# Attention scores in four array quadrants, and weight casts of the opening ordered behind the cast of h

## The chip, the cores and the metric

The kernel runs as one program on one core of a Trainium2 chip. The metric is the device time of one execution in microseconds (us); lower is better. Times of several executions are given as their median.

## The reference, cut to what matters

One layer of a hybrid decoder on 512 tokens of width 2048, all in float32: a conditioning vector scales and shifts the normalized input, one wide projection feeds two branches (sliding-window attention and a gated delta rule), and the branches are merged and projected back.

```python
mod = silu(c) @ w_ada + b_ada                       # 2048 -> 3 x 2048
shift, scale, gate = split(mod, 3)
h = rms_norm(x, norm_w) * (1 + scale) + shift       # 512 x 2048
aq, ak, av, ag, d_qkv, dz, db, da, mg_a, mg_b = split(h @ w_in)

# attention: 32 query heads, 4 key/value heads, head size 64, window of 128 tokens
aq, ak = rope(rms_norm(aq)), rope(rms_norm(ak))
s = einsum(q, k_of_this_and_the_previous_block) / 8 # blocks of 128 queries, 256 keys
s = where(0 <= q_pos - k_pos < 128, s, -inf)        # 128 keys are valid for each query
p = exp(s - m); denom = sum(p) + exp(sink - m)
a_out = (p / denom) @ v * silu(ag)

# gated delta rule: beta = sigmoid(db), g from da, 64-token chunks (not touched)
y = sigmoid(mg_a) * (a_out @ w_o_swa) + sigmoid(mg_b) * (dn_out @ w_o_dn)
return x + gate * (y @ w_out)
```

## The kernel before, in words

**Products.** TensorE does every large product with `float32r` operands: each matrix is split into a high part (a cast to `float32r`) and a low part (what the cast left off), and a product is three matmuls of 128x512, high by high, high by low and low by high (`mm3`, lines 259, 260 and 261). Weights come in halves of up to 1024 columns: `split_half` casts the raw half on ScalarE (`whi`, line 61) and subtracts on VectorE (`wlo`, line 62). Three pairs of `whi` and `wlo` and two raw buffers exist. Matmuls of plain float32 operands are run by the hardware in two passes each, so the profile counts two instructions for each of them.

**The opening** (`startup`). It walks over the 16 slices `kt` of the model width, called steps here. For a step it needs `shift` and `scale` of 128 channels. Each is a sum over 2048 conditioning inputs: TensorE does one of the two in even steps (and in the last), by 16 matmuls of 32 columns (line 449) and a column sum (line 455); VectorE does the rest (`wa`, line 458), so one sum in an even step and two in an odd one. ScalarE makes from both `sh` (lines 468 and 471), from it `h` (line 475), and casts that to `hh` (line 476). VectorE subtracts to get `hl` (line 480). Then TensorE adds the step's products into seven banks: two tiles of attention values (`v`), a 64-column tile with the inputs of beta and the decay (`ba`), and four key tiles of the delta rule (`k`). So a step has 21 matmuls. Its weights are half of a `w_st` block of 1664 columns: 832 columns per step. The sums' weights, 2 MB for each step, come from HBM all along.

**What sets the order.** A scheduler of the framework puts the instructions of each engine in a fixed order when the kernel is built, and each engine works through its own list; across engines only semaphores order the work. `behind(a, b)` forces `a` to come later than `b` in that list. In the kernel before, the low parts of the weights (`wlo`) are put behind the step's last VectorE sum; the casts `whi` are free, and the scheduler puts them where a buffer is free.

**Attention** (`attention`, `group`, `attend`). Its small work is laid between the large products of the attention's own query and gate channels, so that TensorE never stops. For each of 4 key/value heads and each of 4 blocks of 128 tokens, `attend` makes the scores of 8 query heads (two pairs `pp`, in each two tiles `S`, one for each half `e` of the partitions), picks for each query its 128 valid keys out of the own and the previous block with a mask (lines 1424, 1426, 1429), and takes maximum, exponential and sum. The trick of the kernel: exactly 128 keys are valid for a query, so both blocks' scores share one 128x128 tile. It is transposed (`pP`), multiplied by two 0/1 masks `parts` into `pT` of the previous and the own block (line 1464), and multiplied by the values into `O` (line 1474). Score matmuls have 64 rows and 128 columns of stationary queries; `O` has 128 rows and 64 columns of stationary values for each head.

## Time and profile before

| | before |
|---|---|
| times of three executions | 2849.0 (median), 2845.32, 2851.39 us |
| the profiled execution | 2842.31 us, span of its profile 2840.5 us |
| TensorE (PE) busy | 2812.2 us, 99% of the span |
| VectorE (DVE) busy | 1940.2 us, 68% |
| ScalarE (ACT) busy | 1195.2 us, 42% |
| GpSimd (POOL) busy | 146.9 us, 5% |
| DMA | 603.30 MB, mean 212 GB/s |
| stretch of the opening's products | about 31 to 125 us |
| stretch of the attention's small work | about 572 to 1021 us |

Busy times are sums over instructions of an engine; a PE that is busy may still work at less than its peak, because an instruction's record runs from its start to its modelled end and matmuls overlap. So the distance from one start to the next tells what a matmul costs. PEld is the loading of stationary operands, which overlaps PE.

### The profile page before, as it was taken

The numbers are of one execution on the slowest core, as the hardware profiler recorded it, in microseconds if no ns is written. First come the engines' busy times: TensorE is split into PE (matmuls) and PEld (weight loads), VectorE is DVE, ScalarE is ACT, GpSimd is POOL, SyncE is SP. The second block draws the span as 40 slices with busy tenths as digits, with TensorE's granted clock in tenths as the row PEclk, the third lists the DMA queues.
The fourth block names the chain that finished last, engine by engine and source line by source line (L and its number), as shares of the span: only waits on it lengthen the run. The fifth ranks groups of instructions, "written<-read, shape, count | busy, mean of one in ns | idle before, by whom it ended". The sixth has DMA issues, their size and how long they took to land.

```text
span 2840.5 us, 38583 instructions
## 1 busy us (share of the span) xinstructions
PE 2812.2 (99%) x14312; PEld 2305.0 (81%) x14312; DVE 1940.2 (68%) x3142; ACT 1195.2 (42%) x2452; POOL 146.9 (5%) x124
## 2 busy tenths in 40 slices
PE   8999999999999999999999999999999999999999
PEld 5788888887787888888888888888888888888887
DVE  7866776867757666778766666666656766664676
ACT  5555443244454343433434333333334554432443
POOL 0010100100000010000001000000000000000000
PEclk9999999999999999999999999999999999999999
DMA  9878764322244253366777666666646887885684
GB/s 404 333 230 238 255 223 143 110 91 92 80 118 137 87 167 105 116 209 218 243 259 262 231 223 241 230 231 235 242 167 233 300 311 246 303 276 179 245 312 172
DMA packets 228368, 603.30 MB, mean 212 GB/s; under 512 B 76210, under 2 KB 102450, under 8 KB 187858
## 3 DMA queue, kind: packets, MB, share of 16 engines
q1 hardware_dynamic: 228180, 600.83, 62.2%
q8 instruction: 113, 1.85, 0.3%
q14 instruction: 75, 0.61, 0.1%
HBM read 480.35 MB, written 118.17 MB: 211 GB/s over the span
## 4 chain that ended last, share of the span: by engine, by line
PE 94%; DVE 2%; DMA 2%; ACT 1%; issue 1%; SPq 0%; POOL 0%; DVEq 0%; ACTq 0%; POOLq 0%
PE mm L259 22%; PE mm L261 21%; PE mm L260 21%; PE m L260 5%; PE m L259 5%; PE m L261 5%; PE S L1416 1%; PE pv L960 1%; PE O L1474 1%; PE pod L979 1%; PE pod L978 1%; PE pod L975 1%; PE pp L950 1%; DMA E<-g_rows 1%; PE k L259 1%; PE k L260 1%
## 5 line engine op out<-in xcount | busy, mean ns | idle before, releaser
L259 PE MATMUL mm<-hh,whi 128*128 128x512 f32 x2784 | 1129.1, 406 | 0.0
L261 PE MATMUL mm<-hh,wlo 128*128 128x512 f32 x2784 | 1089.2, 391 | 0.0
L260 PE MATMUL mm<-hl,whi 128*128 128x512 f32 x2784 | 1086.4, 390 | 0.0
L62 DVE TENSOR_TENSOR wlo<-raw,whi 128x1024 fp32r<-128x1024 f32 (+1 forms) x532 | 653.2, 1228 | 438.1 <-ACT whi L61 432.4
L61 ACT CAST whi<-raw 128x1024 fp32r<-128x1024 f32 (+1 forms) x532 | 555.9, 1045 | 838.3 <-PE mm L260 595.5
L261 PEld LDWEIGHTS mm<-hh,wlo 128*128 128x128 f32 x2784 | 522.5, 188 | 113.8 <-issue 0.4
L259 PEld LDWEIGHTS mm<-hh,whi 128*128 128x128 f32 x2784 | 523.4, 188 | 111.7 <-issue 10.6
L260 PEld LDWEIGHTS mm<-hl,whi 128*128 128x128 f32 x2784 | 524.0, 188 | 100.8 <-issue 1.6
L1225 DVE TENSOR_TENSOR q<-q,q 128x1024 f32<-128x1024 f32 x96 | 124.8, 1300 | 0.7 <-issue 0.6
L773 ACT ACTIVATE E<-E,neg_g 128x128 f32<-128x128 f32 x256 | 80.9, 394 | 90.5 <-POOL E L767 78.9
L810 DVE TENSOR_TENSOR A<-A,atmp 128x62 f32<-128x62 f32 (+30 forms) x124 | 109.2, 881 | 0.4
L802 DVE TENSOR_TENSOR atmp<-A 128x62 f32<-128x62 f32 (+30 forms) x124 | 107.4, 866 | 0.3
L907 POOL TENSOR_TENSOR qe<-qe,yq 128x512 f32<-128x512 f32 x32 | 55.6, 1755 | 920.1 <-DMA qe<-eg_rows 532.2
L980 ACT COPY osb<-pod 128x256 f32<-128x256 f32 x64 | 23.8, 372 | 152.6 <-PE pod L979 152.6
L767 POOL TENSOR_SCALAR_AFFINE_SELECT E<-E 128x512 f32<-128x512 f32 x64 | 59.3, 941 | 433.2 <-DMA E<-g_rows 241.5
L962 ACT COPY vn<-pv 128x256 f32<-128x256 f32 x64 | 23.8, 372 | 124.4 <-PE pv L960 124.4
L631 DVE SCALAR_TENSOR_TENSOR yv<-mm,convh,yv 128x511 f32<-128x511 f32 (+2 forms) x96 | 71.2, 742 | 1.1
L967 DVE TENSOR_SCALAR vs<-vn,kd 128x128 f32<-128x128 f32 x96 | 23.1, 283 | 58.3 <-ACT vn L962 58.3
L1444 ACT ACTIVATE sm<-sm,mx,rs 128x128 f32<-128x128 f32 x128 | 61.5, 482 | 3.0 <-DVE mx L1439 3.0
L990 DVE SCALAR_TENSOR_TENSOR S<-S,egl,pod 128x128 f32<-128x128 f32 x64 | 19.2, 342 | 51.0 <-ACT junk L983 51.0
L636 ACT ACTIVATE th<-yv 128x512 f32<-128x512 f32 x32 | 20.2, 631 | 76.3 <-DVE yv L631 73.7
L458 DVE SCALAR_TENSOR_TENSOR wa<-wa,silu_cb 128x2048 f32<-128x2048 f32 x22 | 50.1, 2283 | 0.0
(438 smaller groups left out, 3661.4 us busy)
## 6 DMA issues: line engine op xcount, KB each, us to landing
raw<-in_w_ch SPq DMA_DIRECT2D x158, 1024.0 KB
wa<-in_w_ada_ss SPq DMA_DIRECT2D x32, 1024.0 KB
q<-in_w_od SPq DMA_DIRECT2D x64, 512.0 KB
g_d<-q SPq DMA_DIRECT2D x64, 512.0 KB
raw<-g_d SPq DMA_DIRECT2D x32, 1024.0 KB
raw<-in_w_od SPq DMA_DIRECT2D x24, 1024.0 KB
gw<-in_w_ada_gate SPq DMA_DIRECT2D x16, 1024.0 KB
E<-g_rows SPq DMA_DIRECT2D x64, 256.0 KB
```

The lines of the kernel that those rows point to most:

```text
L61: h = self.nc.scalar.copy(out=hi, in_=src)
L62: l = self.nc.vector.tensor_tensor(out=lo, in0=src, in1=hi.bitcast(F32), op=ALU.subtract)
L259: nc.tensor.matmul(ps, lhsT=wh, rhs=xh, start=first, stop=False)
L260: nc.tensor.matmul(ps, lhsT=wh, rhs=xl, start=False, stop=False)
L261: self.last_mm = nc.tensor.matmul(ps, lhsT=wl, rhs=xh, start=False, stop=last)
L631: nc.vector.scalar_tensor_tensor(out=y[:, s:], in0=ps[:, : T - s], scalar=w[:, j : j + 1], in1=y[:, s:], op0=ALU.mult, op1=ALU.add)
L767: self.last_mask = self.nc.gpsimd.affine_select(out=E, in_=E, pattern=[[0, NTB], [1, P]], compare_op=ALU.is_ge, fill=NEG, base=0, channel_ ...
L773: self.nc.scalar.activation(E[:, c, :], E[:, c, :], AF.Exp, bias=self.neg_g[:, c, h : h + 1])
L802: eng.tensor_tensor(out=t, in0=A[:, m : m + 1, m + 1 :].to_broadcast([P, m, n]), in1=A[:, :m, m : m + 1].to_broadcast([P, m, n]), op=ALU.mult,
L810: self.behind(eng.tensor_tensor(out=A[:, :m, m + 1 :], in0=A[:, :m, m + 1 :], in1=t, op=ALU.add))
L1225: self.behind(nc.vector.tensor_tensor(out=q[f], in0=q[x], in1=q[y], op=ALU.add))
L1444: nc.scalar.activation(t, t, AF.Exp, scale=r[:, h : h + 1], bias=mx[:, h : h + 1], accum_out=den[:, h : h + 1])
```

## The change

Five edits, made together:

1. **`ba` in two matmuls.** The columns of `w_st` are put in another order, so that `ba` is last. For the 832-column halves the low part of the 64 `ba` columns is written behind the high part into the same tile `whi` (columns 832 to 895). One matmul of 128 columns then makes high by high in partitions 0 to 63 and low by high in 64 to 127; a second one of 64 columns adds high by low. The two halves are added later in `gates`, by one more VectorE instruction. A step has 20 matmuls instead of 21.
2. **The split of those halves.** Instead of one subtraction of 832 columns, VectorE does one of 768 and one of 64.
3. **The order of the split.** After the first step, the cast `whi` of a step's weights is put behind the cast `hh` of the same step on ScalarE, and both subtractions behind the step's last VectorE sum.
4. **Scores in quadrants.** For the three later blocks of tokens, each score matmul (64 rows, 128 columns, 256 keys) becomes two with 64 rows, 64 columns and 192 keys, one for each half `u` of the queries, which write partitions 0 to 63 and 64 to 127. The scores that both halves have in the same columns are copied at once; two predicated copies of 64 partitions follow instead of one of 128.
5. **Values for four heads.** `O` is made with 512 columns at a time, one matmul for each half `e` and each block of keys (4 in a later block of tokens instead of 16), with the same stationary values. `pT` of the own block is now the transposed tile less `pT` of the previous block, so one mask is left.

```diff
@@ split_half
+            src = raw[:, (n % 2) * w : (n % 2 + 1) * w]
+            if w < 1024:
+                h = self.nc.scalar.copy(out=hi[:, :w], in_=src)
+                sub = lambda out, s: self.nc.vector.tensor_tensor(
+                    out=out, in0=src[:, s], in1=hi[:, s].bitcast(F32), op=ALU.subtract
+                )
+                wide, ba = slice(0, 6 * P), slice(6 * P, w)
+                l = sub(lo[:, wide], wide)
+                low = (l, sub(hi[:, w : w + 2 * VH], ba))
...
             if self.split_behind:
-                self.behind(l, self.split_behind)
+                self.behind(h, self.split_behind[0])
+                for i in low if self.split_behind[1] else ():
+                    self.behind(i, self.split_behind[1])
@@ startup, products
-            for ps, o, n in outs:
+            for i, (ps, o, n) in enumerate(outs):
+                if i == 2:
+                    pair = [(P, x[0]), (2 * VH, x[1])]
+                    for m, xm in pair[::-1] if l else pair:
+                        nc.tensor.matmul(
+                            acc_ba[:m], lhsT=wh[:, 6 * P : 6 * P + m], rhs=xm, start=f and m == P, stop=l and m == P
+                        )
@@ startup, the loop over kt
-            self.split_behind = last_sum.get(kt + 1)
+            self.split_behind = (made["h"], last_sum.get(kt + 1))
@@ gates
-        nc.vector.tensor_copy(out=bd, in_=pb)
+        nc.vector.tensor_copy(out=bd, in_=pb[:, :, 0 : 2 * VH])
+        nc.vector.tensor_tensor(out=bd, in0=pb[:, :, 2 * VH :], in1=bd, op=ALU.add)
@@ attend, scores
-                        nc.tensor.matmul(
-                            ps[:, j, k0:], lhsT=qs[2 * pp + j][b, isl], rhs=kd[b, (i - 1) * P + k0 : (i + 1) * P],
-                            start=True, stop=True,
-                        )
+                        for u in range(2):
+                            rr = slice(u * HD, (u + 1) * HD)
+                            o = u * HD
+                            nc.tensor.matmul(
+                                ps[rr, j, HD - o : 256 - o], lhsT=q[b, i * P + o : i * P + o + HD],
+                                rhs=kd[b, (i - 1) * P + o : (i - 1) * P + o + 192], start=True, stop=True,
+                            )
...
-                        nc.vector.copy_predicated(out=t, mask=mask.bitcast(I32).unsqueeze(1).to_broadcast(wide), data=ps[:, :, :P])
+                    for u in range(2 if i else 0):
+                        rr, o = slice(u * HD, (u + 1) * HD), u * HD
+                        nc.vector.copy_predicated(
+                            out=t[rr, :, o : o + HD], mask=self.other[rr].unsqueeze(1).to_broadcast([HD, 2, HD]),
+                            data=ps[rr, :, 192 - 3 * o : 256 - 3 * o],
+                        )
@@ attend, values
-            for p in range(4):
-                for kb in kbs:
-                    for e in range(2):
-                        nc.tensor.matmul(
-                            po[e * HD : (e + 1) * HD, p, :],
-                            lhsT=self.vtok_a[:, i - 1 + kb, n * HD : (n + 1) * HD], rhs=pTs[e, kb][:, p * P : (p + 1) * P],
+            for kb in kbs:
+                for e in range(2):
+                    nc.tensor.matmul(
+                        po[e * HD : (e + 1) * HD].rearrange("d p q -> d (p q)"),
+                        lhsT=self.vtok_a[:, i - 1 + kb, n * HD : (n + 1) * HD], rhs=pTs[e, kb],
```

The order on ScalarE in the opening, steps 10 and 11, before. The numbers tell tiles apart: `h32_814` is `h` of step 10 and `h32_855` of step 11; `whi_848` and `whi_905` are the high weights of steps 10 and 11; `acc_764` and `acc_821` hold the VectorE sums of steps 10 and 11.

```order
L454 COPY adas_781<-ada_157 128x128
L468 ACTIVATE sh_811<-ada_157,b_adaT_112 128x1
L471 ACTIVATE sh_811<-acc_764,bn_154,norm_wT_114 128x1
L61 CAST whi_848<-raw_748 128x832
L475 ACTIVATE h32_814<-xnT_94,sh_811 128x512
L61 CAST whi_905<-raw_748 128x832
L476 CAST hh_76<-h32_814 128x512
L468 ACTIVATE sh_852<-acc_821,b_adaT_112 128x1
L471 ACTIVATE sh_852<-acc_821,bn_154,norm_wT_114 128x1
L475 ACTIVATE h32_855<-xnT_94,sh_852 128x512
L476 CAST hh_76<-h32_855 128x512
```

The same place on ScalarE after the change. `h32_815` and `h32_856` are now `h` of steps 10 and 11, `acc_765` and `acc_822` their sums, and the weights have kept their numbers.

```order
L467 COPY adas_782<-ada_157 128x128
L481 ACTIVATE sh_812<-ada_157,b_adaT_112 128x1
L484 ACTIVATE sh_812<-acc_765,bn_154,norm_wT_114 128x1
L488 ACTIVATE h32_815<-xnT_94,sh_812 128x512
L489 CAST hh_76<-h32_815 128x512
L231 CAST whi_848<-raw_748 128x832
L481 ACTIVATE sh_853<-acc_822,b_adaT_112 128x1
L484 ACTIVATE sh_853<-acc_822,bn_154,norm_wT_114 128x1
L488 ACTIVATE h32_856<-xnT_94,sh_853 128x512
L489 CAST hh_76<-h32_856 128x512
L231 CAST whi_905<-raw_748 128x832
```

Both weight casts stood ahead of `hh` of step 10, the second of them a whole step early; now each stands behind `hh` of its own step, and so behind that step's VectorE sums.

The order on VectorE at the same place, before (`hl` of steps 9, 10 and 11 come from `h32_757`, `h32_814` and `h32_855`).

```order
L458 SCALAR_TENSOR_TENSOR wa_721,acc_764<-wa_721,silu_cb_93 128x2048
L480 TENSOR_TENSOR hl_77<-h32_757,hh_76 128x512
L62 TENSOR_TENSOR wlo_849<-raw_748,whi_848 128x832
L458 SCALAR_TENSOR_TENSOR wa_760,acc_821<-wa_760,silu_cb_93 128x2048
L480 TENSOR_TENSOR hl_77<-h32_814,hh_76 128x512
L458 SCALAR_TENSOR_TENSOR wa_762,acc_821<-wa_762,silu_cb_93 128x2048
L62 TENSOR_TENSOR wlo_906<-raw_748,whi_905 128x832
L458 SCALAR_TENSOR_TENSOR wa_819,acc_862<-wa_819,silu_cb_93 128x2048
L480 TENSOR_TENSOR hl_77<-h32_855,hh_76 128x512
```

VectorE after the change.

```order
L471 SCALAR_TENSOR_TENSOR wa_722,acc_765<-wa_722,silu_cb_93 128x2048
L493 TENSOR_TENSOR hl_77<-h32_758,hh_76 128x512
L232 TENSOR_TENSOR wlo_849<-raw_748,whi_848 128x768
L471 SCALAR_TENSOR_TENSOR wa_761,acc_822<-wa_761,silu_cb_93 128x2048
L493 TENSOR_TENSOR hl_77<-h32_815,hh_76 128x512
L232 TENSOR_TENSOR whi_848<-raw_748,whi_848 128x64
L471 SCALAR_TENSOR_TENSOR wa_763,acc_822<-wa_763,silu_cb_93 128x2048
L232 TENSOR_TENSOR wlo_906<-raw_748,whi_905 128x768
L232 TENSOR_TENSOR whi_905<-raw_748,whi_905 128x64
L471 SCALAR_TENSOR_TENSOR wa_820,acc_863<-wa_820,silu_cb_93 128x2048
L493 TENSOR_TENSOR hl_77<-h32_856,hh_76 128x512
```

VectorE's list is the same but for the added subtractions of 64 columns; the subtraction that reads `whi_905` still follows at once on the last sum into `acc_822`.

The order on TensorE in the attention, one place where values are followed by scores, before (`mm` is a query or gate channel product).

```order
L261 MATMUL mm<-hh,wlo 128x512
L1474 MATMUL O<-pT,vtok_a 64x128 x16
L1416 MATMUL S<-kd_4584,aq 128x256 x4
L259 MATMUL mm<-hh,whi 128x512
L260 MATMUL mm<-hl,whi 128x512
```

The same place after the change.

```order
L274 MATMUL mm<-hh,wlo 128x512
L1509 MATMUL O<-pT,vtok_a 64x512 x4
L1446 MATMUL S<-kd_4587,aq 64x192 x8
L272 MATMUL mm<-hh,whi 128x512
L273 MATMUL mm<-hl,whi 128x512
```

The small matmuls stay at their place between the same products; only their number and their shape change.

More of the change, by code (lines that the diff above doesn't have):

```diff
@@ L228, in split_half @@
             lo = self.whl.tile([P, 1024], F32R, tag="wlo", name="wlo")
-            h, l = self.split(hi[:, :w], lo[:, :w], raw[:, (n % 2) * w : (n % 2 + 1) * w])
+            src = raw[:, (n % 2) * w : (n % 2 + 1) * w]
[7 more added lines that the diff above has]
+                low = (l, sub(hi[:, w : w + 2 * VH], ba))
+            else:
+                h, l = self.split(hi[:, :w], lo[:, :w], src)
+                low = (l,)
             if self.split_behind:
-                self.behind(l, self.split_behind)
+                self.behind(h, self.split_behind[0])
+                for i in low if self.split_behind[1] else ():
+                    self.behind(i, self.split_behind[1])
             self.halves[n] = (hi, lo)
@@ L1298, in attention @@
             nc.sync.dma_start(out=mask, in_=a["k_mask"])
-            self.parts = keep.tile([P, 2, P], F32, name="parts")
-            nc.sync.dma_start(out=self.parts, in_=a["k_parts"])
+            self.part = keep.tile([P, P], F32, name="part")
+            nc.sync.dma_start(out=self.part, in_=a["k_part"])
+            self.other = keep.tile([P, HD], I32, name="other")
+            nc.sync.dma_start(out=self.other, in_=a["k_other"])
             sink = keep.tile([P, QH], F32, name="sink")
@@ L1423, in attend @@
                     if i:
-                        nc.scalar.copy(out=t, in_=ps[:, :, P:])
+                        nc.scalar.copy(out=t, in_=ps[:, :, HD : HD + P])
                     else:
@@ L1462, in attend @@
                     if i:
-                        part = self.parts[:, kb, :].unsqueeze(1).to_broadcast([P, 4, P])
-                        nc.vector.tensor_tensor(out=four(pT), in0=four(pt), in1=part, op=ALU.mult)
+                        part = self.part.unsqueeze(1).to_broadcast([P, 4, P])
+                        if kb:
+                            nc.vector.tensor_tensor(out=pT, in0=pt, in1=pTs[e, 0], op=ALU.subtract)
+                        else:
+                            nc.vector.tensor_tensor(out=four(pT), in0=four(pt), in1=part, op=ALU.mult)
                     elif e:
@@ L1740, in layout @@
     o["k_mask"] = np.where(n[None, :] <= n[:, None], np.float32(0.0), np.float32(NEG))
-    o["k_parts"] = f(np.stack([n[:, None] > n[None, :], n[:, None] <= n[None, :]], 1).astype(np.float32))
+    o["k_part"] = f((n[:, None] > n[None, :]).astype(np.float32))
+    own = n[None, :HD] <= n[:HD, None]
+    o["k_other"] = f(np.concatenate([own, ~own]).astype(np.int32))
     return o
```

23 lines of the change are left out of this document (13 added, 10 removed).

## The prediction

> **What bounds the kernel now.** I read the page first, then the waits of TensorE, then two stretches alone: the opening and the attention.
>
> ```profile
> PE 2812.2 (99%) x14312; PEld 2305.0 (81%) x14312; DVE 1940.2 (68%) x3142; ACT 1195.2 (42%) x2452; POOL 146.9 (5%) x124
> PE 94%; DVE 2%; DMA 2%; ACT 1%; issue 1%; SPq 0%; POOL 0%; DVEq 0%; ACTq 0%; POOLq 0%
> 64.60:108.70 44.10, 44.10 (x309) 33.83 (x305) 39.69 (x41) 22.85 (x44) 0.00 (x0) 1.00 1.01 423
> 560.00:1030.00 470.00, 469.54 (x2637) 372.76 (x2636) 326.94 (x687) 196.02 (x466) 22.43 (x17) 1.00 0.33 105
> ```
>
> The first two are the page's busy times and its chain that ended last; the others are windows (stretch, length, then busy time of PE, PEld, DVE, ACT and POOL, PE clock, DMA share, GB/s). TensorE sets the time: work taken off its list shortens the run, as long as nothing else becomes late. In the attention everything else has room (DVE 327 of 470 us). In the opening it has little: DVE is busy 39.69 of 44.10 us and DMA is full at 423 GB/s. So the opening has to be read instruction by instruction. These are DVE and ACT there (start, duration, the instruction, idle time before it and who ended that):
>
> ```profile
> 83.83 1.02 DVE L62 TENSOR_TENSOR wlo<-raw,whi 128x832 fp32r<-128x832 f32 x1
> 84.77 2.28 DVE L458 SCALAR_TENSOR_TENSOR wa<-wa,silu_cb 128x2048 f32<-128x2048 f32 x1
> 86.98 0.69 DVE L480 TENSOR_TENSOR hl<-h,hh 128x512 fp32r<-128x512 f32 x1
> 88.89 1.02 DVE L62 TENSOR_TENSOR wlo<-raw,whi 128x832 fp32r<-128x832 f32 x1 [1.22 <-ACT whi L61]
> 89.83 2.28 DVE L458 SCALAR_TENSOR_TENSOR wa<-wa,silu_cb 128x2048 f32<-128x2048 f32 x1
> 92.04 0.69 DVE L480 TENSOR_TENSOR hl<-h,hh 128x512 fp32r<-128x512 f32 x1
> 92.64 2.28 DVE L458 SCALAR_TENSOR_TENSOR wa<-wa,silu_cb 128x2048 f32<-128x2048 f32 x1
> 94.86 1.02 DVE L62 TENSOR_TENSOR wlo<-raw,whi 128x832 fp32r<-128x832 f32 x1
> ...
> 83.95 0.39 ACT L471 ACTIVATE sh<-acc,bn,norm_wT 128x1 f32<-128x1 f32 x1 [2.52 <-DVE wa L458]
> 84.37 0.82 ACT L475 ACTIVATE h<-xnT,sh 128x512 f32<-128x512 f32 x1
> 85.22 0.62 ACT L476 CAST hh<-h 128x512 fp32r<-128x512 f32 x1
> 87.70 0.38 ACT L471 ACTIVATE sh<-acc,bn,norm_wT 128x1 f32<-128x1 f32 x1
> 87.98 0.87 ACT L61 CAST whi<-raw 128x832 fp32r<-128x832 f32 x1
> ```
>
> The eight DVE rows are one period of two steps: from the subtraction at 83.83 to the same one at 94.86 is 11.03 us. Its work fills 9.8 us; it waits once, 1.22 us, for a weight cast. PE does not wait at all in this stretch (44.10 of 44.10 us), so PE makes the period.
>
> **The change part by part.**
>
> *Order of the weight casts (edits 2 and 3).* VectorE's list still says: last sum of a step, then at once (odd step) or one `hl` later (even step) the subtraction of the same step's weights. That subtraction reads `whi`, and `whi` is now cast behind `hh` of the same step, which needs that last sum. Before, the odd step's cast was long done, so the row at 83.83 starts as its sum ends. After, VectorE finishes the sum and must wait for a chain on ScalarE, whose length I add from the rows: sum ends 83.83, `sh` 83.95, `h` 84.37, `hh` 85.22 to 85.84, then the cast, 0.87, done at 86.71, and 0.04 until VectorE starts (the cast ending 88.85 and the row at 88.89): 2.92 us. ScalarE starts an independent instruction about 0.1 before the last one ends (`sh` 87.70 and 0.38, the cast at 87.98), so 2.8 is the lower end; I take 2.9. Nothing is left in VectorE's list that could fill it in an odd step; in an even step `hl` (0.60, from 92.04 to 92.64) fills a part.
>
> A sum takes 2.21 (92.64 to 94.86), the subtraction of 832 takes 0.94 (83.83 to 84.77), so 768 columns take 0.87. The 64-column one has no row: it lies between 0.07 (64/832 of 0.94) and 0.15 (the smallest instruction in the opening below); I take 0.13.
>
> ```profile
> L378 DVE TENSOR_SCALAR dnwh<-dnw 128x1 f32<-128x1 f32 x1 | 0.1, 146 | 0.0
> ```
>
> One period of VectorE after the change:
> - odd step: 2.9 wait + 0.87 + 0.13 + 2.21 (sum of the even step) = 6.1;
> - even step: 2.9 (with `hl` inside) + 0.87 + 2.21 (first sum of the odd step) + 0.60 (`hl`) + 0.13 + 2.21 (second sum) = 8.9.
>
> Together 15.0 us instead of 11.03. ScalarE and VectorE now take turns instead of working side by side, and no buffer lets one of them run ahead. PE's own work in a period stays below 11, so PE waits: for `whi` at a step's start and for `hl` after its first six products. The loss is 4.0 us in each of the five periods from step 4 to step 14. In steps 0 to 3 the chain has no weight cast ahead of `hh` any more but still ends in one: between -3 and +3, taken as 0; in the last two PE follows on its own. So +20. I also walked both lists from the first product, row by row with these durations and the buffers' releases: that gives the end of the opening's products at 124.6 us before and at 144.5 after, so +19.9. The trace of before has its last product at
>
> ```profile
> 124.63 0.39 PE L261 MATMUL k<-hh,wlo 128*128 128x512 f32 x1
> ```
>
> so up to 125.0. I take +20; bounds are +10, if half of each wait found cover after all, and +28.
>
> *`ba` in two matmuls (edit 1).* 16 fewer matmuls on PE at 0.23 each:
>
> ```profile
> 95.66 0.40 PE L260 MATMUL k<-hl,whi 128*128 128x512 f32 x1
> 95.89 0.39 PE L261 MATMUL k<-hh,wlo 128*128 128x512 f32 x1
> ```
>
> That is 3.7 us, but in a stretch where PE now waits, so it is worth 0 in the sum. Were PE still the bound, it would be worth up to -3.7, and less if the loads hold it up (first rival). In `gates`, four transposes of 128 instead of 64 rows and one VectorE instruction more: between 0 and +0.6 on PE's path, taken as +0.2.
>
> *Scores in quadrants (edit 4).* Rows of PE: scores of a first block (128 keys), of a later one (256 keys), values followed by scores, and the opening's sums in 32-column tiles; behind each the row that follows it.
>
> ```profile
> 572.25 0.71 PE L1416 MATMUL S<-kd,aq 64*128 64x128 f32 x8
> 572.90 0.50 PE L259 MATMUL mm<-hh,whi 128*128 128x512 f32 x1
> ...
> 642.97 1.13 PE L1416 MATMUL S<-kd,aq 64*128 64x256 f32 x8
> 644.03 0.50 PE L259 MATMUL mm<-hh,whi 128*128 128x512 f32 x1
> ...
> 661.47 1.97 PE L1474 MATMUL O<-pT,vtok_a 128*64 128x128 f32 x32
> 663.36 1.14 PE L1416 MATMUL S<-kd,aq 64*128 64x256 f32 x8
> ...
> 96.67 1.08 PE L449 MATMUL ada<-wa,silu_cr 128*32 128x128 f32 x32
> 97.68 0.73 PE L259 MATMUL v<-hh,whi 128*128 128x512 f32 x2
> ```
>
> Eight passes take 0.65 us with 128 columns and 1.06 with 256. Two row halves run side by side, so there are four turns: (1.06 - 0.65)/(4 x 128) = 0.80 ns a column, and 0.24 us stay for entering and leaving. The 32 passes of the 32-column sums fit this with four side by side: 8 turns x 128 x 0.80 ns + 0.24 = 1.06, and the rows say 1.01. So 16 passes of quadrants, four side by side, are four turns of 192 columns: 0.61 + 0.24 = 0.85, or -0.21. There are 4 heads x 3 blocks x 2 pairs = 24 such groups: -4.9. If the two column halves ran in turn, it would be eight turns, 1.47, and +9.8; that is the other bound. I take -4.9, because the row of four 32-column tiles is nearest.
>
> The Trainium skill ("TensorE: Matmul & The Clock Gate", section "Part 3: Packing small matmuls — row/col tiling") says that matmuls start and end strictly in program order. By that, a matmul's two passes would follow each other in its quadrant, nine turns for a group (1.62 us, +13 in all), and the 32-column sums would need 17 turns, 1.98 us. The trace has 1.01, so it speaks against the rule for such passes, and the sum goes by the trace.
>
> *Values for four heads (edit 5).* The same columns stream: 16 turns of 128 were 1.89 us (661.47 to 663.36), 4 turns of 512 are 1.64 + 0.24 = 1.88. A few groups entered slower, so I take -0.5 over all 16 groups, between 0 and -3.
>
> *VectorE in the attention (edit 4).* 48 predicated copies of 0.43 become 96 smaller ones, between half of it and all of it each: 0 to +21 us of DVE work in 470, hidden behind PE (DVE has 143 us free there); a late maximum would cost PE 1 us here or there.
>
> ```profile
> L1429 DVE COPY_PREDICATED sm<-mask,S x48: 429/435/455, 615.8 to 1001.5; 128x256 f32<-128x256 int32 x48
> ```
>
> **Sum.** +20 + 0.2 - 4.9 - 0.5 = +14.8 us on the profiled execution's 2842.3, so 2857.1. That execution lies 6.7 below the median of the three runs (2849.0); 14.8/2840.5 is 0.52%, which makes 2864 of the median. Less than 0.2% (5.7 us) either way is what a measurement of this kernel can hardly tell from no change.
>
> **The rivals.**
>
> *The opening doesn't get slower.* If VectorE's wait for the cast were covered, PE would stay the bound and all edits would pay: -4.9 - 0.5, and between 0 and -3.7 for `ba`. The loads limit that last part:
>
> ```profile
> wa<-in_w_ada_ss SPq DMA_DIRECT2D x32, 1024.0 KB
> raw<-in_w_st SPq DMA_DIRECT2D x8, 832.0 KB
> ```
>
> Two steps need four and one of them, 5.05 MB, 11.9 us at 423 GB/s, already more than the 11.03 that PE takes from its lead. So about -7: 2842, faster. For it speaks that PE doesn't wait before although VectorE works 9.8 of 11.03 us; against it, that the wait lies in two lists that are worked through in order. It decides where a period costs less than 11.03 + 5.4/5 = 12.1 us. Chance 0.09.
>
> *Quadrants in turn.* No row here shows four quadrants at work at once; the four side by side were 32-column tiles with all 128 rows. Then +20 + 9.8 - 0.3 = +29: 2879. Chance 0.05.
>
> *The clock falls.* PE would wait some 4 us in each period, in pieces of 1.3 to 2.4 us. In the opening's second step this happened after a wait of 1.71 us:
>
> ```profile
> 40.26 0.51 PE L259 MATMUL v<-hh,whi 128*128 128x512 f32 x1 [1.71 <-ACT hh L476]
> ...
> 41.58 0.63 PE L261 MATMUL v<-hh,wlo 128*128 128x512 f32 x1
> 42.01 0.63 PE L259 MATMUL v<-hh,whi 128*128 128x512 f32 x1
> ...
> 43.72 0.63 PE L260 MATMUL ba<-hl,whi 128*64 128x512 f32 x1
> ```
>
> Products then start 0.43 apart instead of 0.23, until the last such row at 43.72. Such a stretch of some 3 us costs about 1.6; two in a period fit into PE's waits, a third adds 1.6 in each of five periods: +8, 2872. Chance 0.10. The Trainium skill (the same page, section "Why this matters for your kernels") warns of idle gaps above about 3 us only; by it this rival is out and the sum stands. The row with 1.71 us speaks against relying on that.
>
> **How the numbers follow.** The sum has 0.76 and the three rivals 0.09, 0.05 and 0.10. The range goes from 2853 (the opening's loss at its lower bound, +4.8) to 2873 (the clock's case), which leaves out the first two rivals and some of the sum's tails. Slower by over 0.2%: 0.88, from the sum without its low tail and two rivals. Faster: 0.08, the first rival with `ba` worth something. Within: 0.04.
>
> **What would show it.** Right: in the opening a period near 15 us, DVE's wait for ACT `whi` up from 1.2 to some 5 us a period, PE waiting there for `whi` and `hl`, the opening's products ending near 145 us, DMA below full; in the attention score rows of 16 passes in 0.85 us. Wrong: a period near 11, which would mean that VectorE's wait was covered; score rows of 1.4 us or more; or PE rows 0.43 us apart all through the opening.

## The result, and the profile after

The changed kernel takes 2869.98 us (median of 4 runs, 2868.3 to 2871.11); the kernel before, run beside it, takes 2847.16 us (4 runs). The ratio is 1.0079, 95% interval 1.0066 to 1.0091: slower, by 22.8 us. The forecast was 2864 (2853 to 2873). The profiled execution took 2870.80 us with a span of 2869.0, near its own median; the one of before (2842.31) is 4.9 us below its median, so the two traces differ by more than the medians do, by 28.5 us.

The page of the changed kernel, its busy times and the chain that ended last:

```profile
PE 2815.6 (98%) x14152; PEld 2286.6 (80%) x14152; DVE 1955.2 (68%) x3207; ACT 1195.4 (42%) x2452; POOL 143.3 (5%) x124
PE 85%; DVE 6%; DMA 4%; ACT 3%; issue 1%; SPq 1%; POOL 0%; DVEq 0%; ACTq 0%; POOLq 0%
```

PE had 94% of the chain; now it has 85, and DVE has 6 instead of 2. PE's busy time has hardly changed (2815.6 against 2812.2 us), so what the run is longer by are waits, for VectorE above all. The waits of PE in the opening (29 to 145 us; total, number and the longest of each) say where:

```profile
PE v L273 <- DVE hl L493: 13.9, 8, 2.1
PE v L272 <- ACT whi L231: 5.6, 9, 1.0
PE v L272 <- ACT hh L489: 2.1, 1, 2.1
```

and so does a window over five of its periods, with the columns of the windows in the prediction:

```profile
61.60:136.40 74.80, 60.30 (x406) 44.82 (x407) 50.24 (x61) 30.62 (x58) 0.00 (x0) 0.95 0.73 286
```

PE works 60.3 of 74.8 us, DMA moves 286 GB/s where it moved 423. One period of VectorE, and ScalarE in its second half (start, duration, instruction, idle time ahead and its releaser):

```profile
72.69 0.96 DVE L232 TENSOR_TENSOR wlo<-raw,whi 128x768 fp32r<-128x768 f32 x1 [2.13 <-ACT whi L231]
73.57 2.28 DVE L471 SCALAR_TENSOR_TENSOR wa<-wa,silu_cb 128x2048 f32<-128x2048 f32 x1
...
75.78 0.69 DVE L493 TENSOR_TENSOR hl<-h,hh 128x512 fp32r<-128x512 f32 x1
76.38 0.22 DVE L232 TENSOR_TENSOR whi<-raw,whi 128x64 fp32r<-128x64 f32 x1
76.52 2.29 DVE L471 SCALAR_TENSOR_TENSOR wa<-wa,silu_cb 128x2048 f32<-128x2048 f32 x1
...
81.55 0.96 DVE L232 TENSOR_TENSOR wlo<-raw,whi 128x768 fp32r<-128x768 f32 x1 [2.74 <-ACT whi L231]
82.43 0.22 DVE L232 TENSOR_TENSOR whi<-raw,whi 128x64 fp32r<-128x64 f32 x1
82.56 2.29 DVE L471 SCALAR_TENSOR_TENSOR wa<-wa,silu_cb 128x2048 f32<-128x2048 f32 x1
...
84.77 0.69 DVE L493 TENSOR_TENSOR hl<-h,hh 128x512 fp32r<-128x512 f32 x1
...
87.60 0.96 DVE L232 TENSOR_TENSOR wlo<-raw,whi 128x768 fp32r<-128x768 f32 x1 [2.14 <-ACT whi L231]
...
78.85 0.39 ACT L484 ACTIVATE sh<-acc,bn,norm_wT 128x1 f32<-128x1 f32 x1 [2.66 <-DVE wa L471]
79.27 0.82 ACT L488 ACTIVATE h<-xnT,sh 128x512 f32<-128x512 f32 x1
80.11 0.62 ACT L489 CAST hh<-h 128x512 fp32r<-128x512 f32 x1
80.64 0.88 ACT L231 CAST whi<-raw 128x832 fp32r<-128x832 f32 x1
```

From 72.69 to 87.60 is 14.91 us. VectorE's sum ends at 78.8; ScalarE then runs `sh`, `h`, `hh` and the weight cast one after another, and VectorE starts its subtraction at 81.55, the moment the cast ends. While one works the other waits. The last product of the opening starts at

```profile
143.71 0.39 PE L274 MATMUL k<-hh,wlo 128*128 128x512 f32 x1
```

so they end at 144.1, 19.1 us later than before (125.0).

In the attention the score groups are shorter, as 16 passes of quadrants (start, duration, and the row behind):

```profile
633.69 0.88 PE L1446 MATMUL S<-kd,aq 64*64 64x192 f32 x16
634.50 0.50 PE L272 MATMUL mm<-hh,whi 128*128 128x512 f32 x1
```

A group holds PE for 0.81 us (633.69 to 634.50) instead of 1.06. The predicated copies as a group (shortest, median and longest in ns):

```profile
L1459 DVE COPY_PREDICATED sm<-other,S x96: 279/301/313, 635.0 to 1024.7; 64x128 f32<-64x128 int32 x96
```

These are 96 of 0.301 us, 28.9 us in all, 8.0 more than the 48 of 0.435. VectorE's busy time, in which instructions that overlap count once, grows by more over the same products, from 319.3 us (570.1 to 1030.3) to 334.9 (589.6 to 1052.6). And the stage isn't shorter. To see it, take one and the same product (the n-th `mm<-hh,whi` in the program, 2,784 in either kernel) and ask how much later it starts than before: the one at before's 570 us starts 19.4 us later, the one at 1030 us starts 22.2 us later. The attention costs 2.8 us, where -5.4 was forecast. PE's waits for it from 580 to 1052 us:

```profile
PE pP L319 <- DVE sm L1485: 2.2, 3, 1.6
PE O L1509 <- DVE pT L1498: 1.1, 2, 0.7
PE O L1509 <- DVE pT L1500: 0.6, 2, 0.3
```

and the window from 893.4 to 900.2:

```profile
893.40:900.20 6.80, 6.80 (x31) 2.96 (x31) 6.43 (x11) 2.91 (x5) 0.38 (x1) 0.50 0.05 10
```

PE waits 3.9 us for VectorE, where before has one wait of 0.3; and for 6.8 us its granted clock is 0.50 (the column behind the engines), with PE busy throughout, which is up to 3.4 us lost. Together that is 7.0 of the 8.2 us missing.

### The profile page after: what moved, and what is told of

Its sections match the earlier page's. It is cut to its first block, busy times and chain, and to the rows that moved or that the text cites. A ratio compares the mean times of both kernels' runs of the same rounds, so it can differ in the third digit from the quotient of the medians.

```text
span 2869.0 us, 38356 instructions
## 1 busy us (share of the span) xinstructions
PE 2815.6 (98%) x14152; PEld 2286.6 (80%) x14152; DVE 1955.2 (68%) x3207; ACT 1195.4 (42%) x2452; POOL 143.3 (5%) x124
## 4 chain that ended last, share of the span: by engine, by line
PE 85%; DVE 6%; DMA 4%; ACT 3%; issue 1%; SPq 1%; POOL 0%; DVEq 0%; ACTq 0%; POOLq 0%
PE mm L272 21%; PE mm L274 20%; PE mm L273 20%; PE m L273 5%; PE m L272 5%; PE m L274 4%; DVE wa L471 2%; DVE wlo L62 1%; DMA E<-g_rows 1%; PE pv L980 1%; PE pod L999 1%; PE O L1509 1%; PE pod L998 1%; PE pod L995 1%; PE pp L970 1%
## 5 line engine op out<-in xcount | busy, mean ns | idle before, releaser
L62 DVE TENSOR_TENSOR wlo<-raw,whi 128x1024 fp32r<-128x1024 f32 x516 | 634.9, 1232 | 425.9 <-ACT whi L61 408.0
L61 ACT CAST whi<-raw 128x1024 fp32r<-128x1024 f32 x516 | 541.3, 1050 | 829.0 <-PE mm L273 593.3
L987 DVE TENSOR_SCALAR vs<-vn,kd 128x128 f32<-128x128 f32 x96 | 23.2, 284 | 58.3 <-ACT vn L982 58.3
```

Of the source, the lines that this page charges most:

```text
L61: h = self.nc.scalar.copy(out=hi, in_=src)
L62: l = self.nc.vector.tensor_tensor(out=lo, in0=src, in1=hi.bitcast(F32), op=ALU.subtract)
```

## The experiments

All were run beside the kernel before; its medians lay between 2844.6 and 2845.1 (the changed kernel's row is the result above, beside 2847.16). For each run the columns of this table are read as above: the end of the opening's products, how far the attention (before's 570 to 1030 us) became longer in the trace, the time at half clock in it, and a chain on VectorE and ScalarE: from the last score matmul of a block's heads to the first division of their exponentials, median over the 12 later blocks. A dash is a value that the text doesn't use.

```
run                 products end  attention  half clock  chain   median us  ratio (95%)
before                  125.0         -          0        8.62     2845      1
changed kernel          144.1       +2.8        6.8       9.98     2869.98   1.0079 (1.0066-1.0091)
casts_free              122.8       +2.5        3.4      10.01     2846.51   1.0007 (0.9998-1.0016)
order_only              144.8        0.0         0        8.62     2866.42   1.0076 (1.0063-1.0088)
casts_a_step_early      123.8       +0.8         0        9.98     2847.25   1.0010 (0.9999-1.0020)
attention_only            -         +2.3        3.4       9.98     2849.22   1.0017 (1.0008-1.0026)
scores_only               -         +2.6         0        9.97     2850.32   1.0016 (1.0008-1.0025)
values_only               -         -0.3         0        8.62     2846.49   1.0008 (0.9999-1.0017)
one_copy                  -         -4.5         0        8.16     2844.67   1.0000 (0.9991-1.0009)
half_norm                 -         +5.8        6.8       9.89     2850.67   1.0018 (1.0009-1.0027)
half_norm_before          -         +0.1         0        8.62     2844.48   1.0000 (0.9991-1.0009)
one_wide_copy             -         -5.2         0        8.67     2839.24   0.9978 (0.9969-0.9986)
extra_off_chain           -         -4.3         0        8.72     2840.71   0.9983 (0.9974-0.9992)
extra_in_chain            -         -1.0         0        9.95     2842.53   0.9995 (0.9985-1.0006)
```

**The opening.** First the change without its cast order (`casts_free`):

```diff
 if self.split_behind:
-    self.behind(h, self.split_behind[0])
     for i in low if self.split_behind[1] else ():
```

> The changed kernel with one line less: the weight casts of the opening are not put behind the cast of h; all other edits stay. Theory (the cast order makes the whole loss of the opening): the period of two steps falls from about 15 us to 11 or less, the opening's products end between 121.3 (the two-matmul ba paid in full, 3.7 us) and 125.0 us (held by the loads) instead of 144.1; of the attention nothing changes against the changed kernel (+2.5 us against before, by the products' start times), so the run is between 1 us below and 3 us above before: about 2848 us. Rival (the narrow subtraction or the new order of ba takes part in the loss): the products end later than 127 us. Second rival (the attention's surplus in the changed kernel is the clock's fall at 893 us alone): the attention takes 5 us less than before, 2840 us.

The products end at 122.8, inside the forecast of the theory. The window over five periods here (58.61 to 113.15 us):

```profile
58.61:113.15 54.54, 54.52 (x403) 42.03 (x403) 50.60 (x61) 29.01 (x55) 0.00 (x0) 1.00 0.99 413
```

PE is busy in 54.52 of 54.54 us and DMA is back at 413 GB/s; VectorE does the same work (50.60 us) in 54.5 instead of 74.8 us. Nothing but the missing overlap made the loss. It also shows what the two-matmul `ba` is worth once PE is the bound: 2.2 us at the end of the products, less than the 3.7 of its matmuls. But the whole run is not faster than before, since the attention keeps its +2.5.

Then the cast order alone, in the kernel before (`order_only`):

```diff
-                self.behind(l, self.split_behind)
+                self.behind(h, self.split_behind[0])
+                if self.split_behind[1]:
+                    self.behind(l, self.split_behind[1])
...
-            self.split_behind = last_sum.get(kt + 1)
+            self.split_behind = (made["h"], last_sum.get(kt + 1))
```

> The kernel before with the cast order alone: each weight cast of the opening is put behind the cast of h, ba stays in three matmuls and the subtraction in one piece, the attention is as before. Theory: period near 14.9 us, the opening's products end near 144 us, +19 us behind them, and nothing else: 2847 + 19 + up to 2 for what the clock does = 2866 to 2868 us. Rival (the clock or something behind the opening pays too): more than 2870 us; rival (the split of the subtraction is needed for the loss): the products end before 138 us, under 2860 us.

The products end at 144.8, the attention is unchanged, 2866.42 us: +21.3, ratio 1.0076. The split subtraction has no part in it. Its waits in the opening read like those of the changed kernel:

```profile
PE v L262 <- DVE hl L482: 12.3, 8, 2.0
PE v L261 <- ACT whi L61: 3.0, 7, 0.9
PE v L261 <- ACT hh L478: 2.1, 1, 2.1
```

Last, is it the fixed place, or the chain within one step? The cast is put behind the `hh` of the step before its own (`casts_a_step_early`):

```diff
+            made["before"] = made["h"]
             nxt = kt + 1 < KT and adaln(kt + 1)
...
-            self.split_behind = (made["h"], last_sum.get(kt + 1))
+            self.split_behind = (made["before"], last_sum.get(kt + 1))
```

> The changed kernel with all its edits, but each weight cast of the opening is put behind the cast of h of the step before its own. Theory (it is the chain last sum, sh, h, hh, cast, subtraction of one and the same step that makes VectorE and ScalarE take turns): period near 11 us, the opening's products end at 122 to 125 us as with free casts, 2846 to 2850 us. Rival (any fixed place behind an hh costs): the products end later than 130 us, over 2853 us.

Products end at 123.8, 2847.25 us. A cast with a fixed place costs next to nothing (the products end 1.0 us later than with free casts) as long as it doesn't hang on the sum that VectorE has just finished. It is the chain of one and the same step.

**The attention.** The attention's edits alone, in the kernel before, and the same with the values left as they were (`attention_only`, `scores_only`):

> The kernel before with the attention's edits alone (scores in quadrants, two smaller predicated copies, values for four heads); the opening is as before. The prediction's sum: -5.4 us, 2842 us. Theory now (the score groups are shorter, 0.81 against 1.06 us, but VectorE, which has 8 us more of predicated copies, is late for the transposes and the values, and PE waits): PE gains 6 us on the score groups and loses 4 to 8 us in waits on VectorE's sm and pT: -2 to +3 us, 2845 to 2850 us. Rival (the loss was the clock's fall behind one such wait, by chance of that execution): the products behind the attention start 4 to 6 us earlier than before.

> As the run with the attention's edits alone, but the values stay in 32 matmuls of one head each. The prediction's terms: -4.9 us (2842 us). Theory (VectorE's smaller copies make it late, whatever the values do): within 1 us of the run with both edits, with PE waits on sm and pT as there. Rival (the joined values wait longer, since each of their 512-column matmuls holds PE's order for its whole input): PE doesn't wait for pT here, and the run is 3 to 5 us shorter than the one with both.

Both are slower than before by some 4 to 5 us (ratios 1.0017 and 1.0016), both make the attention longer in the trace (+2.3 and +2.6). So the loss comes with the scores' edit, and it is no chance of one execution; the run without any stretch at half clock there has it too. The rival of the second, that the joined values wait, is out. (This run has the new way to make `pT` too; the run with one wide copy below keeps that and loses nothing.) The values alone (`values_only`), 8 matmuls of 512 columns in place of 32:

> The kernel before with the values for four heads alone (8 matmuls of 512 columns in place of 32 of 128); the scores as before. The prediction's term: -0.5 us, 0 to -3. Theory: VectorE's work is unchanged, so no new waits: within 1.5 us of before, 2844.5 us. Rival (the joined values keep PE in order for their whole input and make it wait): +2 us or more, with O waiting for pT.

Attention -0.3 us in the trace, whole run not to be told from before (ratio 0.9999 to 1.0017): the term of -0.5 holds as far as the stage shows it.

Now VectorE's side. In one run the second copy of each pair is left out (`one_copy`):

```diff
-                    for u in range(2 if i else 0):
+                    for u in range(1 if i else 0):
```

> The kernel before with the attention's edits, and of each pair of predicated copies the second is left out (so the lower 64 queries keep a wrong part of their scores): 48 copies of 0.30 us less, 14.4 us of VectorE's work, 6.5 less than before has. Theory (VectorE's added work and its longer chain to the maximum make PE wait): PE's waits on sm and pT in the attention fall from 4.1 us to under 1, the products behind the attention start 3 to 6 us earlier than before (attention's edits alone: 2.7 later), about 2841 us. Rival (the waits come from the quadrants or the joined values, not from the copies): within 1.5 us of 2849.

The attention becomes 4.5 us shorter than before's, 6.8 less than with both copies: the copies are the cause. The median is 4.5 us lower than with both copies, but only equal to before, where 2841 was expected. Behind the attention the profiled execution lost some 7 us again (its products start 3.7 us earlier than before's at 1030 us and 3.6 later near the end), in waits and at half clock that other runs show too, in stages that no edit touches (below). Whether the other executions lost their gain in the same way isn't shown.

Is it the amount of VectorE's work, or its place? Half of the divisions were moved to ScalarE, with the attention's edits (`half_norm`) and, as a control, without them (`half_norm_before`):

```diff
             for h in range(8):
                 t = sm[h]
-                nc.vector.tensor_scalar(out=t, in0=t, scalar1=den[:, h : h + 1], scalar2=None, op0=ALU.mult)
+                if h % 2:
+                    nc.scalar.activation(t, t, AF.Identity, scale=den[:, h : h + 1])
+                else:
+                    nc.vector.tensor_scalar(out=t, in0=t, scalar1=den[:, h : h + 1], scalar2=None, op0=ALU.mult)
```

> The kernel before with the attention's edits, both copies, and the division of the scores of every odd head moved from VectorE to ScalarE: 64 x 0.28 = 18 us less on VectorE, some 64 x 0.4 = 26 us more on ScalarE (which is busy 196 of 470 us there). The chain to the maximum is as long as in the run with the attention's edits alone. Theory, amount (VectorE has too much to do): as with one copy, waits under 1.5 us, products behind the attention 2 to 5 us earlier than before, about 2843 us. Rival, chain (two copies one behind the other in the chain from the scores to the maximum): waits stay near 4 us, 2848 us.

> The kernel before with nothing changed but the division of every odd head on ScalarE: the control to the run above. Theory: before has only 0.3 us of waits for sm in the attention and a few late pT, so it gains 0 to 2 us: 2843 to 2845 us. Rival (any relief of VectorE shortens the attention by itself): more than 3 us faster; rival (ScalarE's weight casts come late): slower by 2 us or more.

Over the same products VectorE is now busy for 324.5 us, 11 less than with the attention's edits alone (335.5), though still 5 more than before (319.3). The attention is 5.8 us longer, the worst of all (6.8 us at half clock are up to 3.4 of it), where the theory of the amount had it shorter. I had thought the amount likelier; it didn't help to take a good part of it away. The control changes nothing (+0.1). What stayed is the chain up to the division, 9.89 us. In the kernels so far every chain near 10 us goes with a longer attention, every chain of 8.2 to 8.6 doesn't.

Why is it 1.4 us longer in the median, when the copies of a block's last four heads, four instead of two, make only a part of that? The first later block of the first heads on VectorE, before:

```profile
619.79 0.78 DVE L1429 COPY_PREDICATED sm<-mask,S 128x256 f32<-128x256 int32 x2 [0.46 <-ACT sm L1424]
...
621.64 0.17 DVE L1437 TENSOR_TENSOR es<-sink,mx 128x8 f32<-128x8 f32 x1
621.84 0.17 DVE L1439 TENSOR_SCALAR mx<-mx 128x8 f32<-128x8 f32 x1
621.92 1.10 DVE L810 TENSOR_TENSOR A<-A,atmp 128x902 f32<-128x902 f32 x1
626.01 0.17 DVE L1448 TENSOR_TENSOR den<-den,es 128x8 f32<-128x8 f32 x1 [3.00 <-ACT sm L1444]
626.21 0.20 DVE L1449 RECIPROCAL den<-den 128x8 f32<-128x8 f32 x1
626.45 1.47 DVE L1452 TENSOR_SCALAR sm<-sm,den 128x128 f32<-128x128 f32 x7
```

and after:

```profile
639.21 0.94 DVE L1459 COPY_PREDICATED sm<-other,S 64x128 f32<-64x128 int32 x3
...
641.68 0.17 DVE L1470 TENSOR_TENSOR es<-sink,mx 128x8 f32<-128x8 f32 x1
641.76 1.09 DVE L830 TENSOR_TENSOR A<-A,atmp 128x902 f32<-128x902 f32 x1
642.77 0.17 DVE L1472 TENSOR_SCALAR mx<-mx 128x8 f32<-128x8 f32 x1
647.00 0.17 DVE L1481 TENSOR_TENSOR den<-den,es 128x8 f32<-128x8 f32 x1 [4.06 <-ACT sm L1477]
647.20 0.20 DVE L1482 RECIPROCAL den<-den 128x8 f32<-128x8 f32 x1
647.32 1.03 DVE L822 TENSOR_TENSOR atmp<-A 128x882 f32<-128x882 f32 x1
648.27 1.65 DVE L1485 TENSOR_SCALAR sm<-sm,den 128x128 f32<-128x128 f32 x8
```

The copies themselves cost 0.62 us here: from the first copy to `es` it is 1.85 us before and 2.47 after. (Their durations would say 4 x 0.301 - 2 x 0.435 = 0.33, but before, each overlaps with the next instruction.) And the order of VectorE's list has changed. The step `A<-A,atmp` of a stage that has nothing to do with the attention stood behind the negated maximum, where VectorE waits for the exponentials anyway and the step is free. Now it stands ahead of it, and the exponentials, which need that maximum, start 0.9 us later for it. A second one, `atmp<-A`, stands between the reciprocal and the divisions, another 0.8. From the first copy to the first division it is 6.66 us before and 9.06 after. So 0.6 us of copies came with 1.7 us of other work in the chain.

That is the block where the order changed most. Of the 12 later blocks, four have a chain that is 1.8 to 2.8 us longer than before's, six one that is 0.7 to 1.2 longer, and two a shorter one. The longest wait of PE in the attention, the 1.59 us just ahead of the fall at 893.4, follows a block without a displaced step; there a small step of VectorE took 1.15 us instead of 0.17, while GpSimd worked on `aq`:

```profile
885.73 1.15 DVE L1468 TENSOR_TENSOR mx<-mx,sink 128x8 f32<-128x8 f32 x1
885.55 1.31 POOL L1292 TENSOR_TENSOR aq<-aq,cos 128x512 f32<-128x512 f32 x1 [82.52 <-DVE mx L1464]
```

All six runs with two copies for each pair have such a step in this block and the wait (1.5 to 1.8 us) behind it. Before has such a step too (1.25 us at 671.82), without a wait behind it. How much of the loss is owed to the copies themselves, to the displaced steps and to this one, no run separates.

To take that away and keep the shorter score groups, each pair of copies becomes one again, over all queries and 128 keys, on the kernel with free casts (`one_wide_copy`). The second half's data lie 192 columns before the first's, so the data are read with a negative step; the mask is a table of 128 x 128, and three score banks are kept and cleared once:

```diff
-                    for u in range(2 if i else 0):
-                        rr, o = slice(u * HD, (u + 1) * HD), u * HD
+                    if i:
+                        four = lambda x: x.rearrange("p j (c k) -> p j c k", k=HD)
                         nc.vector.copy_predicated(
-                            out=t[rr, :, o : o + HD], mask=self.other[rr].unsqueeze(1).to_broadcast([HD, 2, HD]),
-                            data=ps[rr, :, 192 - 3 * o : 256 - 3 * o],
+                            out=four(t), mask=four(self.other.unsqueeze(1).to_broadcast(wide)), data=four(ps)[:, :, 3::-3, :],
                         )
```

> The changed kernel with the casts free as in the first run, and with each pair of predicated copies joined into one of all 128 queries and 128 keys (the data read with a negative step, 192 columns back for the second half; three score banks are kept and cleared once, since the copy also reads columns that it doesn't use). One copy should take 0.43 us as before's, so chain and amount of VectorE are as before. Theory (the longer copies cost the attention what the score groups gained): PE's waits on sm and pT under 1.5 us, the attention takes 4 to 6 us less than before, the products behind it start 6 to 9 us earlier than before, 2838 to 2841 us, faster than both. Rival (PE runs into VectorE's pace as soon as its own groups are shorter, copies or not): attention -2 to +1 us, 2843 to 2846 us.

2839.24 us, ratio 0.9978 (0.9969 to 0.9986): faster than both kernels. The attention is 5.2 us shorter than before's, near the -4.9 - 0.5 of the sum, now that VectorE's price is gone; the opening, with free casts, ends 2.4 us earlier. Some of it is paid back at once: right behind the attention PE waits 1.5 us for `yq` of the next stage, as it does for 0.6 to 1.4 us in most of the runs with the shorter score groups and not at all before. Its page:

```profile
PE 2804.7 (99%) x14152; PEld 2282.3 (81%) x14152; DVE 1942.6 (69%) x3162; ACT 1196.5 (42%) x2452; POOL 146.1 (5%) x124
PE 94%; DVE 2%; DMA 2%; ACT 1%; issue 1%; POOL 0%; SPq 0%; DVEq 0%; ACTq 0%
```

the group of copies:

```profile
L1463 DVE COPY_PREDICATED sm<-other,S x48: 429/440/455, 611.7 to 992.5; 128x256 f32<-128x256 int32 x48
```

and PE's only wait for VectorE there:

```profile
PE pP L318 <- DVE sm L1488: 0.9, 1, 0.9
```

Last, amount and place against each other: the same kernel with four small multiplications that nobody reads in each later block, once behind the block's last `pT` (`extra_off_chain`) and once between the last maximum and its scaling (`extra_in_chain`):

```diff
+            for _ in range(4 if i else 0):
+                ins = nc.vector.tensor_tensor(out=self.extra, in0=self.part[:, 0:8], in1=self.part[:, 8:16], op=ALU.mult)
+                self.behind(ins, last_pT)
```

In the second run the last line is `self.behind(ins, last_max)`, and the scaling of the maximum is put behind the last `ins`.

> The run with one wide copy, and four small VectorE multiplications (0.17 us, nobody reads them) in each of the 12 later blocks, behind the block's last pT: 8 us of VectorE's work as the two copies had added, but not between the scores and the maximum. Theory, chain: less than 1.5 us slower than the run with one wide copy, no new waits on sm. Rival, amount: 4 us or more slower.

> The same four small multiplications in each later block, but between the last maximum of the scores and its scaling, so 0.7 us longer from the scores to the weights. Theory, chain: PE waits on sm and pT 3 to 6 us longer than with one wide copy, 3 to 7 us slower. Rival, amount: the same time as with them off the chain.

The same 7.8 us of work (48 x 0.16; 4.7 and 5.0 us of busy time) costs the attention 0.9 us off the chain (-4.3 against -5.2) and 4.2 us in it (-1.0). The chain is 8.72 and 9.95 us. PE's waits for `sm` and `pT` grow less than expected, from 0.9 to 2.3 us instead of by 3 to 6; the rest lies in the groups of values, during which PE counts as busy. In the medians the two are 1.8 us apart, with intervals that overlap (0.9974 to 0.9992 and 0.9985 to 1.0006), so this rests on the stage in the traces. There the amount alone is out: VectorE is busy for 325.9 us over the same products with the work off the chain, more than the 324.5 of the run with half of the divisions, and the one attention is 4.3 us shorter than before's, the other 5.8 longer. In the chain the added work does what the two copies did:

```profile
616.41 0.76 DVE L1472 TENSOR_TENSOR extra<-part 128x8 f32<-128x8 f32 x4
...
617.49 0.17 DVE L1479 TENSOR_TENSOR es<-sink,mx 128x8 f32<-128x8 f32 x1
617.57 1.09 DVE L829 TENSOR_TENSOR A<-A,atmp 128x902 f32<-128x902 f32 x1
618.58 0.17 DVE L1481 TENSOR_SCALAR mx<-mx 128x8 f32<-128x8 f32 x1
```

The added 0.76 us and the displaced step of 1.09 both stand ahead of the negated maximum. How much of the loss is the added work itself, and how much the order that came with it, no run here separates.

## Why the prediction was right, and where its size was off

- **Order of the weight casts, +20.** Right, and by its own steps. Period 15.0 forecast, 14.91 measured; VectorE's waits for the cast 2.74 and 2.13 in a period (2.9 less `hl` in the even step); products ending at 144.5, measured 144.1. That the loss is this edit's alone is shown by `order_only` (+21.3 us in the medians) and `casts_free` (none), and that the chain of one step is its mechanism by `casts_a_step_early`.
- **`ba` in two matmuls, 0 in the sum, up to -3.7 with PE as the bound.** Right: 0 where PE waits, -2.2 in `casts_free`.
- **Gates, +0.2.** Not to be seen: the products around 160 us start 20.4 us later, at 240 us 19.2. All six runs with the two-matmul `ba` gain 1.2 to 2.4 us between these places, no other does; before has a wait of 2.3 us for `kT` there that the changed kernel hasn't. Which part of the edit does it is open.
- **Scores in quadrants, 0.85 us a group.** Right: 0.81. Four quadrants stream side by side; in turn a group would be 1.47, by the prediction's 0.80 ns a column. The Trainium skill's rule of strict program order ("TensorE: Matmul & The Clock Gate", "Part 3: Packing small matmuls — row/col tiling"), applied to the two passes of each product, would have given 1.62 by the prediction's estimate; the row of 633.69 speaks against it for these passes.
- **Values, -0.5.** Right: -0.3 in `values_only`.
- **VectorE in the attention, taken as 0.** This is the term that was mis-sized: it is +8.2 us in the profiled execution (up to 3.4 of it at half clock), and 6.2 in `casts_a_step_early`, whose attention ran at full clock. The amount was bounded well (8.0 us by the copies' durations, 15.5 by busy time, in 0 to 21), but "hidden behind PE (DVE has 143 us free there)" read the room off the stage's busy share. Most of those 143 us lie where VectorE waits for weight casts (56.5 us) and for the exponentials (39.3); the copies lie in the chain ahead of the exponentials, where PE has its transposes and values next. And the price wasn't that of the copies alone: the chain grew by 1.4 us in the median where they account for 0.6, since in some blocks other steps moved into it. That order was there to be read before any run, from VectorE's list.
- **The sum.** +14.8 forecast; +19 from the opening and +2.8 from the attention are 22, and the medians say +22.8. With the missing term in it the sum closes. That the time lay inside the range is in part luck: the range's upper end came from the clock's case, and what used up the room was VectorE in the attention.
- **The clock.** As a rival it was half right. It fell twice in the opening's middle (at 70.8 and 101.5 us, 3.4 us each) and the products still ended where the sum had them; it fell again at 893.4, behind a wait of 1.59 us for `sm`, for 6.8 us. In the attention it fell only in kernels with the longer chain, and not in all of them (not in `scores_only`, `casts_a_step_early` and `extra_in_chain`). The Trainium skill (the same page, "Why this matters for your kernels") speaks of gaps above about 3 us; here shorter ones did it.

The 28.5 us between the two traces hold some 5 us more, lost behind 1060 us (the delay grows from 23.2 to 28.3). `order_only` and `attention_only` show the same there (+6.0 and +5.4), `one_wide_copy` and `half_norm_before` don't (+0.7 and -0.5), though none of them touches those stages. I put it down to the execution, not to the change; that isn't shown.

## What to carry to other kernels

Price an engine's added work by the slack of the chain in which it stands, not by the share of the stage in which the engine is idle. When work in a planned list grows, look at what the planner now puts between its steps: with 0.6 us of copies more, an unrelated step of 1.09 us stood in the chain, and that is visible in the order before anything runs. And two engines that each wait for the other's result of the same step add up; one step of distance brought the overlap back.

## What the runs showed of the hardware

- Four 64 x 64 quadrants with two-pass F32 products stream at once: 16 passes of 192 columns in 0.81 us (in turn 1.47, at the prediction's 0.80 ns a column).
- The granted clock falls to half in stretches of 3.41 us (6.8 is two of them), and they lie on a common grid: in the changed kernel they begin at 29.8, 70.8, 101.5, 893.4 and 1644.3 us, which are 12, 9, 232 and 220 times 3.413 us apart. A wait of 1.6 to 2.1 us was enough in some places and not in others: behind 61 us the opening has eight waits for `hl` (1.3 to 2.1 us), and two, of 1.85 and 1.83 us, were followed by a fall.
- A predicated copy on half the partitions and half the elements (64 x 128) takes 0.30 us, the whole one (128 x 256) 0.44: splitting it in two saved nothing, it cost 0.62 us in the four heads of 619.79 and 639.21. The whole one reads its data with a negative step at the same price.
- A small VectorE step (128 x 8) that takes 0.17 us took 1.15 while GpSimd worked on `aq` (885.55 to 886.86).
